# Three edits around the RWKV rounds of a hybrid encoder: a table of retention steps per round, a joint output norm of both token halves, and other tiles for the first output weights

## The chip, the cores and the metric

The kernel runs on one core of a Trainium2 chip. The metric is the device time of one execution in microseconds (us). Engines are named as in the profile: PE is TensorE (PEld its weight loads), ACT ScalarE, DVE VectorE, POOL GpSimd, SP SyncE, which here only issues DMAs.

## What is computed

Two layers. Each projects the normalised tokens, runs three groups of heads side by side (retention, RWKV-7, differential attention), multiplies the concatenated result by an output matrix and adds a SwiGLU. The change touches the end of the first two groups and the start of the output projection:

```python
for l in range(DEPTH):                                   # DEPTH = 2, 1024 tokens, 1024 features
    proj = rms_norm(x, mix_norm_g[l]) @ w_in[l]
    y_ret  = retention_mixer(...)    # head_group_norm(y_fwd + y_bwd) * silu(g), 6 heads of 64
    y_rwkv = rwkv7_mixer(...)        # a scan in each direction, then:
        # y = head_group_norm(ys[0] + flip(ys[1]), ln_w, ln_b)
        # return (y + bonus) * gate,   gate = sigmoid(xg @ g1) @ g2
    y_diff = diff_attention(...)
    x = x + concatenate([y_ret, y_rwkv, y_diff], -1) @ w_out[l]
    x = x + (silu(rms_norm(x) @ w_gate[l]) * (rms_norm(x) @ w_up[l])) @ w_down[l]

def head_group_norm(y, w, b, eps):   # over the 64 features of a head
    yn = (y - mean(y)) * rsqrt(mean((y - mean(y))**2) + eps)
    return yn * w + b
```

## The kernel before

Tokens lie along the free dimension in two halves of 512, features on 128 partitions, so a pair of heads fills a tile. Dense products are made of three matmuls each, with every operand split into a high part (ACT copies it, L185) and a low part (the rest, by DVE or POOL, L188).

**The rounds.** `rwkv` (L858) runs the RWKV scan of a layer in rounds w = -2 to 11. There are three pairs of heads, each with four blocks (two halves by two directions), so twelve blocks; round w runs the second half of block w and the first half of block w+1. A round has 16 slots, and eight recurrence steps start in it, one in every second slot (four in rounds -1 and 11). One step (`rwkv_rec`) hops between engines: PE makes `x`, ACT copies it to `U`, PE makes `ns`, ACT scales it to the new state `S`, PE adds to the output `y`. In the same slots the round advances generators "beside" the recurrence: products and inverses of later blocks (`rwkv_prep`, `rwkv_inv`, `rwkv_key`, `rwkv_ready`), the output norm `rwkv_fin` of a finished half, and the retention group `ret_all`. Each generator has a rate, in steps (`yield`s) per round; those but the retention are run out at the end of the round in one go. The retention keeps `RSTEP = 10` steps per round and takes 42 steps for each of its three pairs. At the end the program order of PE, ACT, DVE and POOL inside the rounds is fixed by dependencies, so each of these engines works its list in the written order; an instruction that waits holds all behind it.

**The norms.** `head_norm` (L808) squares `y` on ACT, sums over heads on PE (`vps`), and on ACT takes `Ln` and `Exp` with scale -0.5 for the reciprocal root; then DVE multiplies and ACT applies weight and bias (Identity). `Ln` and the other functions of the rounds use different tables of ACT, so a table load stands before and after each `Ln`. `head_norm` has two callers: the retention, once for each pair, with both halves (tiles `ryT`, `rt`), and `rwkv_fin` (L832), once for each pair and half (tiles `y`, `fq`). `rwkv_fin` also loads the bonus `bo` and the gate input `gl`, makes the gate on PE (`gps`), and writes the half to DRAM (`mixed`). Half 1 of pair p is normed in round 4p+3, half 0 in round 4p+4; the last half 0 comes after the rounds. The tiles `y`, `bo`, `gl` and the four of the bonus share a ring of four buffers.

**The output projection.** `out_blocks` (L1363) loads the eight rows of `mixed` for half 1, splits them (`mixl` to `hh` and `hl`), and works eight output blocks `cb` by both halves into PSUM tiles `aps`. The weights of blocks 0 and 1 are loaded by POOL's DMA queue into the tiles `wr` of pool W, split there by ACT (`whh`) and POOL (`wll`). W's memory is that of tiles the rounds use; `wr`'s load waits until those are read for the last time. Pool F (18 buffers of 128 x 512) holds the residual rows `x`.

Of the kernel before, what the change touches and what calls it, by code (L numbers as in the profile page):

```python
# [27 lines left out]
RSTEP = 10  # L28
# [149 lines left out]
class Net:  # L178
# [630 lines left out]
    def head_norm(self, y, eps, w, b, q):  # L809
# [14 lines left out]
        self.act(q, q, AF.Exp, scale=-0.5)  # L824
        yield
        for i in range(n):
            self.tt(q[:, sl[i]], y[i], q[:, sl[i]], ALU.mult)
            self.act(q[:, sl[i]], q[:, sl[i]], AF.Identity, scale=w, bias=b)

    def rwkv_fin(self, l, st, half):  # L830

        nc = self.nc  # L832
        p = st["p"]
        pp = self.par[l][:, P_PAIR + p * PP:P_PAIR + (p + 1) * PP]
        sl = slice(half * 512, half * 512 + 512)
        yield
        lg = self.Y.tile([128, 128], F32, tag="lg", name="lg")
        nc.sync.dma_start(out=lg, in_=self.ia["lora"][l, :, 1920 + p * 128:2048 + p * 128])
        bo = self.ring("bo")
        nc.sync.dma_start(out=bo, in_=self.bod[p][:, sl])  # L840
        gl = self.ring("gl")
        nc.sync.dma_start(out=gl, in_=self.lod[2][:, sl])
        q = self.Y.tile([128, 512], F32, tag="fq", name="fq", bufs=2)
        yield
        yield from self.head_norm([st["y"][half]], self.eps64, pp[:, Q_LNW:Q_LNW + 1], pp[:, Q_LNB:Q_LNB + 1], q)
        yield 1
        ps = self.bank([128, 512], "gps")
        self.mm(ps, lg, gl)
        self.tt(q, q, bo, ALU.add)
        yield  # L850
        self.tt(q, q, ps, ALU.mult)
        self.free(ps)
        nc.sync.dma_start(out=self.mixed[3 + p][:, sl], in_=q)

    def rwkv(self, l):
# [32 lines left out]
        ret = [self.ret_all(l), RSTEP, 0, 0]  # L888
        first = len(self.nc.cur_bb.bb.instructions)
        active, outs = [], []  # L890
        for w in range(-2, 12):
# [18 lines left out]
            if w >= 0 and j == 3:  # L910
                beside.append([self.rwkv_fin(l, sts[p], 1), 10, 0, 0])
            if w > 0 and j == 0:
                beside.append([self.rwkv_fin(l, sts[p - 1], 0), 10, 0, 0])
            if w > -2:
                beside.append(ret)
            else:
                next(ret[0])
# [34 lines left out]
        run(ret[0], self.rwkv_fin(l, sts[2], 0))  # L952
# [412 lines left out]
    def out_blocks(self, l):  # L1365
# [283 lines left out]
```

## Time and profile before

| what | us |
|---|---|
| median of three runs (3480.74 to 3483.1) | 3482.06 |
| the profiled execution, as timed | 3490.52 |
| its span, first to last instruction | 3488.7 |
| rounds of layer 0, round -1 to the last recurrence step | 572 to 950 |
| rounds of layer 1 | 2296 to 2671 |

The numbers of the views below are those of the profiled execution. A round is cut where ACT copies the first `U` of its recurrence steps. In a timeline row, the square bracket is the time in which the engine stood idle just before, and what ended it. PEclk is the clock that TensorE was granted, as a share of 2.4 GHz. A windows row gives start:end and length of the stretch, then the busy time of PE, PEld, DVE, ACT and POOL, each with its count of instructions, then PEclk, the busy share of the DMA engines and GB/s. The two layers run the same program; the rows below are of layer 1.

### The profile page before, as it was taken

The numbers are of one execution on the slowest core, as the hardware profiler recorded it, in microseconds if no ns is written. First come the engines' busy times: TensorE is split into PE (matmuls) and PEld (weight loads), VectorE is DVE, ScalarE is ACT, GpSimd is POOL, SyncE is SP. The second block draws the span as 40 slices with busy tenths as digits, with TensorE's granted clock in tenths as the row PEclk, the third lists the DMA queues.
The fourth block names the chain that finished last, engine by engine and source line by source line (L and its number), as shares of the span: only waits on it lengthen the run. The fifth ranks groups of instructions, "written<-read, shape, count | busy, mean of one in ns | idle before, by whom it ended". The sixth has DMA issues, their size and how long they took to land.

```text
span 3488.7 us, 71259 instructions
## 1 busy us (share of the span) xinstructions
PE 3209.4 (92%) x29148; PEld 2596.5 (74%) x29148; DVE 1994.8 (57%) x3805; ACT 1568.5 (45%) x2993; POOL 824.5 (24%) x724
## 2 busy tenths in 40 slices
PE   6999799988798999999989997998987999999997
PEld 4778587876676888878867776877766778887886
DVE  4699525676348555542338884176754585555433
ACT  4576444656534333332236664356555333333322
POOL 2222130000022545422122221200001144544220
PEclk9999799998899999999999998999988999999999
DMA  5454324433242222283044433344324322224721
GB/s 176 147 149 123 111 103 157 138 112 114 95 174 73 76 90 77 85 286 118 27 161 130 149 109 123 107 142 157 116 95 162 114 73 79 79 82 140 238 73 49
DMA packets 214928, 419.43 MB, mean 120 GB/s; under 512 B 23972, under 2 KB 59812, under 8 KB 214564
## 3 DMA queue, kind: packets, MB, share of 16 engines
q1 hardware_dynamic: 191288, 376.83, 32.8%
q0 software_dynamic: 10640, 14.95, 1.9%
q10 hardware_dynamic: 12672, 23.07, 1.7%
q8 instruction: 230, 3.77, 0.4%
q14 instruction: 98, 0.80, 0.1%
HBM read 314.06 MB, written 100.70 MB: 119 GB/s over the span
## 4 chain that ended last, share of the span: by engine, by line
PE 75%; DVE 11%; ACT 7%; DMA 3%; issue 2%; POOL 1%; SPq 0%; DVEq 0%; ACTq 0%; POOLq 0%
PE sp L194 22%; PE dps L194 14%; PE dn L194 13%; PE aps L194 5%; PE ns L194 2%; ACT L185 2%; PE y L194 2%; DMA wr<-in_w_in_dram 1%; PE pv L194 1%; PE tps L1247 1%; DVE pt L1217 1%; PE s L194 1%; PE btp L194 1%; PE pps L194 1%; PE yps L194 1%
## 5 line engine op out<-in xcount | busy, mean ns | idle before, releaser
L188 POOL TENSOR_TENSOR wll<-wr,whh 128x512 fp32r<-128x512 f32 x400 | 541.4, 1356 | 1452.7 <-ACT whh L185 1262.0
L185 ACT ACTIVATE whh<-wr 128x512 fp32r<-128x512 f32 x416 | 260.8, 630 | 643.2 <-PE dn L194 169.3
L194 PE MATMUL dps<-hh,whh 128*128 128x512 f32 x960 | 388.0, 405 | 0.5 <-ACT whh L185 0.3
L194 PE MATMUL dps<-hl,whh 128*128 128x512 f32 x960 | 384.4, 400 | 2.8 <-DVE hl L188 2.7
L194 PE MATMUL dps<-hh,wll 128*128 128x512 f32 x960 | 384.0, 400 | 0.7 <-POOL wll L188 0.6
L194 PE MATMUL sp<-hl,whh 128*128 128x512 f32 x704 | 278.6, 396 | 2.0 <-DVE hl L188 2.0
L194 PE MATMUL dn<-hh,whh 128*128 128x512 f32 x704 | 275.9, 392 | 4.6 <-ACT hh L185 4.6
L194 PE MATMUL dn<-hl,whh 128*128 128x512 f32 x704 | 277.0, 393 | 2.5 <-DVE hl L188 2.5
L194 PE MATMUL sp<-hh,whh 128*128 128x512 f32 x704 | 276.8, 393 | 1.8 <-ACT hh L185 1.4
L194 PE MATMUL dn<-hh,wll 128*128 128x512 f32 x704 | 275.6, 392 | 0.0
L194 PE MATMUL sp<-hh,wll 128*128 128x512 f32 x704 | 275.0, 391 | 0.0
L188 DVE TENSOR_TENSOR hl<-hidr,hh 128x512 fp32r<-128x512 f32 x144 | 137.5, 970 | 180.7 <-ACT hh L185 178.7
L194 PEld LDWEIGHTS dps<-hl,whh 128*128 128x128 f32 x960 | 183.8, 191 | 48.8 <-DVE hl L188 8.1
L194 PEld LDWEIGHTS dps<-hh,whh 128*128 128x128 f32 x960 | 184.1, 192 | 45.1 <-issue 4.4
L188 POOL TENSOR_TENSOR wll<-ws,whh 128x512 fp32r<-128x512 f32 x120 | 175.6, 1463 | 175.2 <-ACT whh L185 169.1
L194 PE MATMUL sp<-sh,whh 128*128 128x512 f32 x528 | 210.4, 398 | 6.8 <-ACT as L185 6.8
L194 PE MATMUL sp<-sl,whh 128*128 128x512 f32 x528 | 212.1, 402 | 3.0 <-DVE sl L188 2.8
L194 PEld LDWEIGHTS dps<-hh,wll 128*128 128x128 f32 x960 | 183.5, 191 | 39.7 <-issue 2.4
L194 PE MATMUL sp<-sh,wll 128*128 128x512 f32 x528 | 211.7, 401 | 0.0
L185 ACT ACTIVATE whh<-ws 128x512 fp32r<-128x512 f32 x132 | 83.4, 632 | 240.2 <-PE sp L194 138.0
L185 ACT ACTIVATE pt<-pt,mx 128x1024 f32<-128x1024 f32 x128 | 146.9, 1149 | 62.3 <-DVE mx L1221 59.9
L194 PEld LDWEIGHTS dn<-hh,whh 128*128 128x128 f32 x704 | 133.2, 189 | 33.3 <-ACT hh L185 5.4
(277 smaller groups left out, 7193.2 us busy)
## 6 DMA issues: line engine op xcount, KB each, us to landing
hidr<-hid SPq DMA_DIRECT2D x144, 256.0 KB, 5.3
bias<-t SPq DMA_DIRECT2D x64, 512.0 KB, 3.7
wr<-in_w_in_dram SPq DMA_DIRECT2D x120, 256.0 KB, 3.0
wr<-in_w_gate_dram SPq DMA_DIRECT2D x44, 512.0 KB, 3.7
wr<-in_w_up_dram SPq DMA_DIRECT2D x44, 512.0 KB, 3.2
wr<-in_w_down_dram SPq DMA_DIRECT2D x44, 512.0 KB, 4.1
pr<-st SPq DMA_DIRECT2D x56, 256.0 KB, 2.3
lo<-lod SPq DMA_DIRECT2D x48, 256.0 KB, 3.2
```

What stands on the lines that cost most here:

```text
L185: self.nc.scalar.activation(out=out, in_=in_, func=func, **kw)
L188: (eng or self.nc.vector).tensor_tensor(out=out, in0=a, in1=b, op=op)
L194: self.nc.tensor.matmul(out, lhsT, rhs, start=start, stop=stop, **kw)
L1217: nc.vector.tensor_tensor_reduce(out=pt[:, sl], in0=ps, in1=bias[:, sl], scale=1.0, scalar=mx[:, 0:1] if kh else -3.0e38, op0=ALU.add, op1 ...
L1247: nc.tensor.transpose(ps[:, n * 128:(n + 1) * 128], P[0][:, c * 128:(c + 1) * 128], self.ident)
```

## The change

Three edits:

1. The retention's rate becomes a table, `RSTEPS`, one entry for each round from -2 to 11: 10, 10, 9, 9, 8, 10, 12, 12, 12, 7, 20, 24, 8 from round -1 on. `head_norm` is cut into more steps (the `Exp` and the final products of each half have steps of their own), so a retention pair takes 45 steps.
2. `rwkv_fin` takes a tuple of halves. For pairs 0 and 1 both halves are normed together in round 4p+4; round 4p+3 has no norm. Pair 2 keeps its half 1 in round 11 and half 0 after the rounds. `fq` becomes one tile of 1024 columns; the gate matrix `lg` is loaded once for a pair; `bo` and `gl` of the second half are loaded after the first half is done.
3. In `out_blocks` the weights of output blocks 0 and 1 go to four tiles of pool F (`wf`, split to `fh` and `fl`), loaded by POOL's queue and split at a high priority.

```diff
-RSTEP = 10
+RSTEPS = (0, 10, 10, 9, 9, 8, 10, 12, 12, 12, 7, 20, 24, 8)
...
     def head_norm(self, y, eps, w, b, q):
...
             self.act(q[:, sl[i]], ps[i], AF.Ln, scale=1.0 / 64, bias=eps[:, 0:1])
             self.free(ps[i])
-        self.act(q, q, AF.Exp, scale=-0.5)
-        yield
         for i in range(n):
+            yield
+            self.act(q[:, sl[i]], q[:, sl[i]], AF.Exp, scale=-0.5)
+        for i in range(n):
+            yield
             self.tt(q[:, sl[i]], y[i], q[:, sl[i]], ALU.mult)
             self.act(q[:, sl[i]], q[:, sl[i]], AF.Identity, scale=w, bias=b)
 
-    def rwkv_fin(self, l, st, half):
+    def rwkv_fin(self, l, st, halves):
...
+        if halves[0]:
+            lg = st["lg"] = self.Y.tile([128, 128], F32, tag="lg", name="lg")
+            nc.sync.dma_start(out=lg, in_=self.ia["lora"][l, :, 1920 + p * 128:2048 + p * 128])
+            st["q"] = self.Y.tile([128, T], F32, tag="fq", name="fq")
...
+        ld = load(halves[0])
...
+        yield from self.head_norm([st["y"][half] for half in halves], self.eps64, pp[:, Q_LNW:Q_LNW + 1],
+                                  pp[:, Q_LNB:Q_LNB + 1], q)
+        for i, half in enumerate(halves):
+            bo, gl = ld if i == 0 else load(half)
+            t = q[:, i * 512:i * 512 + 512]
+            yield 1
+            ps = self.bank([128, 512], "gps")
+            self.mm(ps, lg, gl)
+            self.tt(t, t, bo, ALU.add)
+            yield
+            self.tt(t, t, ps, ALU.mult)
...
-            if w >= 0 and j == 3:
-                beside.append([self.rwkv_fin(l, sts[p], 1), 10, 0, 0])
+            if w == 11:
+                beside.append([self.rwkv_fin(l, sts[p], (1,)), 10, 0, 0])
             if w > 0 and j == 0:
-                beside.append([self.rwkv_fin(l, sts[p - 1], 0), 10, 0, 0])
+                beside.append([self.rwkv_fin(l, sts[p - 1], (1, 0)), 10, 0, 0])
             if w > -2:
+                ret[1] = RSTEPS[w + 2]
                 beside.append(ret)
...
+        raw = [self.F.tile([128, 4, 128], F32, tag="f", name="wf") for _ in range(4)]
+        for i, r in enumerate(raw):
+            nc.gpsimd.dma_start(out=r, in_=self.ia["w_out"][l, i // 2, :, i % 2 * 4:i % 2 * 4 + 4])
+        with self.tc.high_priority(offset=200000):
+            for i, r in enumerate(raw):
+                hi, lo = self.split(self.F, r, ("f", "f"), eng=nc.gpsimd)
+                w[i // 2] = w.get(i // 2, []) + [(hi[:, k], lo[:, k]) for k in range(4)]
         load(0)
-        for cb in range(2):
-            w[cb] = self.weights(self.ia["w_out"][l, cb], nc.gpsimd)
         load(1)
```

What this does to the order of the engines is shown at three places. The first is ACT in the middle of round 3, of layer 0: `e`, `cs`, `kd` and `WC` belong to the preparation of a later block, `S` and `U` to the recurrence. Before:

```order
L185 ACTIVATE cs<-cs 128x512
L185 ACTIVATE kd<-ta,der_127 128x512
L185 ACT_TABLE_LOAD
L185 ACTIVATE fq<-vps,eps_122 128x512
L185 ACT_TABLE_LOAD
L185 ACTIVATE fq<-fq 128x512
L185 ACTIVATE WC<-e_3467 128x8
L185 ACTIVATE S<-ns,WC 128x64
```

And now:

```order
L185 ACTIVATE cs<-cs 128x512
L185 ACTIVATE kd<-ta,der_127 128x512
L185 ACTIVATE rt<-rt 128x512
L185 ACTIVATE WC<-e_3467 128x8
L185 ACTIVATE S<-ns,WC 128x64
```

The norm of half 1 of pair 0 has left round 3; in its place stands one half's `Exp` of the retention's norm of pair 0, whose `Ln` now stands between the two `lw` at the start of this round and stood at the end of round 2.

The second is DVE from the last product of a round's preparation (`BP`) to the first part of the output sum `y` of round 4, layer 0: `rq`, `rsw` and `rQ` are the rotary products of the retention's pair 1, `N`, `NB`, `TB` and `YB` the inverse of a later block. Before:

```order
L188 TENSOR_TENSOR BP<-srp,c 128x8x64
L188 TENSOR_TENSOR rq<-rq,rsw 128x1024
L188 TENSOR_TENSOR rQ<-rq,rc 64x1024
L639 STREAM_TRANSPOSE N<-NB 128x8x32
L613 STREAM_TRANSPOSE NB<-N 128x1024
L188 TENSOR_TENSOR TB<-NB,YB 128x30
L188 TENSOR_TENSOR YB<-YB,TB 128x2x15
L188 TENSOR_TENSOR rQ<-rq,rc 64x1024
L188 TENSOR_TENSOR y<-y,yT 128x256
```

And now:

```order
L188 TENSOR_TENSOR BP<-srp,c 128x8x64
L639 STREAM_TRANSPOSE N<-NB 128x8x32
L613 STREAM_TRANSPOSE NB<-N 128x1024
L188 TENSOR_TENSOR TB<-NB,YB 128x30
L188 TENSOR_TENSOR YB<-YB,TB 128x2x15
L188 TENSOR_TENSOR rsw<-rsw,rope 128x1024
L188 TENSOR_TENSOR rq<-rq,rope 128x1024
L188 TENSOR_TENSOR y<-y,yT 128x256
```

Two wide products of the retention stand ahead of `y` where three stood.

The third is ACT from the last norm (half 0 of pair 2, behind the rounds) to the first split rows of the output projection, layer 0. Before:

```order
L185 ACTIVATE fq<-y 128x512
L185 ACT_TABLE_LOAD
L185 ACTIVATE fq<-vps,eps_122 128x512
L185 ACT_TABLE_LOAD
L185 ACTIVATE fq<-fq 128x512
L185 ACTIVATE fq<-fq,par_74 128x512
L185 ACTIVATE hh<-mixl 128x512 x6
L185 ACTIVATE whh<-wr 128x512
L185 ACTIVATE hh<-mixl 128x512
L185 ACTIVATE whh<-wr 128x512
```

And now:

```order
L185 ACTIVATE fq<-y 128x512
L185 ACT_TABLE_LOAD
L185 ACTIVATE fq<-vps,eps_122 128x512
L185 ACTIVATE fh<-wf 128x512
L185 ACT_TABLE_LOAD
L185 ACTIVATE fq<-fq 128x512
L185 ACTIVATE fh<-wf 128x512 x2
L185 ACTIVATE fq<-fq,par_74 128x512
L185 ACTIVATE fh<-wf 128x512
L185 ACTIVATE hh<-mixl 128x512 x13
```

The copies of the first weights stand inside the last norm, ahead of all `hh`.

## Rows read from the trace of the kernel before

**Rows 1.** The page: busy time by engine, and the chain that ended last.

```profile
PE 3209.4 (92%) x29148; PEld 2596.5 (74%) x29148; DVE 1994.8 (57%) x3805; ACT 1568.5 (45%) x2993; POOL 824.5 (24%) x724
PE 75%; DVE 11%; ACT 7%; DMA 3%; issue 2%; POOL 1%; SPq 0%; DVEq 0%; ACTq 0%; POOLq 0%
```

**Rows 2.** Windows, rounds 2 to 11 of layer 1: busy PE, PEld, DVE, ACT, POOL; clock.

```profile
2378.20:2410.70 32.50, 29.11 (x850) 24.71 (x846) 18.27 (x54) 22.66 (x53) 0.37 (x4) 1.00 0.48 157
2410.70:2443.00 32.30, 26.51 (x680) 21.63 (x684) 23.18 (x58) 22.27 (x53) 0.00 (x0) 0.89 0.57 175
2443.00:2481.00 38.00, 31.49 (x736) 26.42 (x728) 26.48 (x62) 21.70 (x54) 0.00 (x0) 0.87 0.30 93
2481.00:2509.80 28.80, 28.77 (x769) 24.43 (x765) 25.59 (x60) 16.28 (x47) 0.00 (x0) 1.00 0.35 114
2509.80:2542.40 32.60, 28.94 (x814) 25.46 (x814) 16.82 (x51) 18.30 (x50) 0.37 (x4) 0.97 0.51 171
2542.40:2580.20 37.80, 30.36 (x746) 23.59 (x740) 22.40 (x59) 26.99 (x57) 0.00 (x0) 0.89 0.31 95
2580.20:2609.20 29.00, 24.56 (x652) 21.56 (x646) 22.01 (x52) 16.05 (x41) 0.00 (x0) 0.88 0.18 60
2609.20:2637.70 28.50, 26.97 (x698) 24.19 (x696) 12.47 (x16) 9.66 (x32) 0.00 (x0) 0.94 0.17 59
2637.70:2653.20 15.50, 15.46 (x342) 13.99 (x338) 2.32 (x5) 5.00 (x19) 0.00 (x0) 1.00 0.22 70
2653.20:2671.20 18.00, 10.89 (x114) 6.29 (x108) 5.03 (x9) 13.82 (x22) 0.00 (x0) 0.72 0.20 64
```

**Rows 3.** Timeline of ACT, the norm in round 3.

```profile
2423.64 1.28 ACT L185 ACT_TABLE_LOAD   x1
2424.94 0.69 ACT L185 ACTIVATE fq<-vps,eps 128x512 f32<-128x512 f32 x1
2425.64 1.28 ACT L185 ACT_TABLE_LOAD   x1
...
2427.58 0.29 ACT L185 ACTIVATE S<-ns,WC 128x64 f32<-128x64 f32 x1
```

**Rows 4.** Timeline of PE, the first matmul after four of its waits.

```profile
2410.89 0.48 PE L194 MATMUL ns<-Vd,kT 64*64 64x64 f32 x4 [3.04 <-ACT S L185]
...
2427.92 0.48 PE L194 MATMUL ns<-Vd,kT 64*64 64x64 f32 x4 [3.25 <-ACT S L185]
...
2450.05 0.33 PE L194 MATMUL y3ps<-NB,N 32*32 32x32 f32 x8 [2.68 <-ACT NB L185]
...
2665.84 0.48 PE L194 MATMUL x<-S,AR 64*64 64x64 f32 x4 [4.22 <-ACT S L185]
```

**Rows 5.** Timeline of DVE at the start of round 4.

```profile
2442.01 0.69 DVE L188 TENSOR_TENSOR BP<-srp,c 128x512 f32<-128x512 f32 x1 [2.20 <-PE srp L194]
2442.62 1.22 DVE L188 TENSOR_TENSOR rq<-rq,rsw 128x1024 f32<-128x1024 f32 x1
...
2448.88 0.42 DVE L188 TENSOR_TENSOR y<-y,yT 128x256 f32<-128x256 f32 x1
```

**Rows 6.** Timeline of ACT, the retention's norm in round 7.

```profile
2551.74 1.06 ACT L185 ACTIVATE rt<-rt 128x1024 f32<-128x1024 f32 x1
2554.41 1.50 ACT L185 ACTIVATE rt<-rt,der 128x512 f32<-128x512 f32 x2
```

**Rows 7.** Timeline of PE, eight transposes of the retention.

```profile
2458.76 1.05 PE L194 MATMUL tps<-c,rv 128*128 128x128 f32 x8
```

**Rows 8.** Timelines of PE, ACT and DVE at the start of the output projection.

```profile
2684.70 0.80 PE L194 MATMUL aps<-hh,whh 128*128 128x512 f32 x1 [10.42 <-ACT whh L185]
2686.74 0.80 PE L194 MATMUL aps<-hh,wll 128*128 128x512 f32 x1 [0.82 <-POOL wll L188]
2678.59 0.69 DVE L188 TENSOR_TENSOR fq<-fq,gps 128x512 f32<-128x512 f32 x1
2684.16 8.26 DVE L188 TENSOR_TENSOR hl<-mixl,hh 128x512 fp32r<-128x512 f32 x7 [0.35 <-ACT hh L185]
```

More of the change, by code (lines that the diff above doesn't have):

```diff
@@ L834, in rwkv_fin, with load @@
         pp = self.par[l][:, P_PAIR + p * PP:P_PAIR + (p + 1) * PP]
-        sl = slice(half * 512, half * 512 + 512)
         yield
[L837 to L843, printed above, removed]
-        yield
[L845 to L853, printed above, removed]
+        if halves[0]:
+            lg = st["lg"] = self.Y.tile([128, 128], F32, tag="lg", name="lg")
+            nc.sync.dma_start(out=lg, in_=self.ia["lora"][l, :, 1920 + p * 128:2048 + p * 128])
+            st["q"] = self.Y.tile([128, T], F32, tag="fq", name="fq")
+        lg = st["lg"]
+        def load(half):
+            r = []
+            for name, src in (("bo", self.bod[p]), ("gl", self.lod[2])):
+                t = self.ring(name)
+                nc.sync.dma_start(out=t, in_=src[:, half * 512:half * 512 + 512])
+                r.append(t)
+            return r
+        ld = load(halves[0])
+        q = st["q"]
+        if len(halves) == 1:
+            q = q[:, halves[0] * 512:halves[0] * 512 + 512]
+        yield
+        yield from self.head_norm([st["y"][half] for half in halves], self.eps64, pp[:, Q_LNW:Q_LNW + 1],
[9 more added lines that the diff above has]
+            self.tt(t, t, ps, ALU.mult)
+            self.free(ps)
+            nc.sync.dma_start(out=self.mixed[3 + p][:, half * 512:half * 512 + 512], in_=t)
     def rwkv(self, l):
@@ L887, in rwkv @@
         self.rwkv_open2()
-        ret = [self.ret_all(l), RSTEP, 0, 0]
+        ret = [self.ret_all(l), 0, 0, 0]
         first = len(self.nc.cur_bb.bb.instructions)
@@ L951, in rwkv @@
                 left = [b for b in left if b[2] != -1]
-        run(ret[0], self.rwkv_fin(l, sts[2], 0))
+        run(ret[0], self.rwkv_fin(l, sts[2], (0,)))
         last = {}
```

## The prediction, made before the changed kernel ran

> **What bounds the kernel now.** I read the page first. PE is busy in 92% of the span and 75% of the chain that ended last is PE work [rows 1], so no edit can win more than the time in which PE stands idle, or runs at half clock because it stood idle. None of the three edits removes PE work: they move it, and they move what PE waits for. So the question is where, around the RWKV rounds, PE waits. For this I cut both layers into rounds and asked for busy times in each [rows 2]. The reader should see in each row the length less the PE time. Rounds 5 and 10 have none left (28.80 against 28.77, 15.50 against 15.46, clock 1.00): they are PE's. Rounds 2, 3, 4, 6, 7, 8, 9 and 11 have 3.39, 5.79, 6.51, 3.66, 7.44, 4.44, 1.53 and 7.11 us of idle time, together 39.9 of 293 us, and in most of them the clock is below 1.00 as well. At half clock a matmul takes twice as long, so a wait costs more than its own length: busy time is longer behind it too.
>
> Then I read what ends these waits, on PE's timeline. In rounds 2, 3 and 11 it is the state `S` of ACT: 3.04, 3.25 and 4.22 us [rows 4]. ACT is not full there (22.66 of 32.50, [rows 2]), but in a burst: in round 3 the first table load of the `fq` norm begins at 2423.64 and the next `S` at 2427.58 [rows 3], so for 3.94 us ACT does nothing for the recurrence. PE has about 0.7 us of other work in its list there and waits the remaining 3.25. In round 4 the wait of 2.68 has another cause [rows 4]: ACT makes `NB` late since ACT's list holds a transpose `yT` for DVE's `y`, and DVE reached `y` only at 2448.88, 6.87 us after `BP`, for it had three wide products of 1.22 us of the retention ahead of it [rows 5]. In round 7 the retention's norm of pair 1 is the burst: `Exp` 1.06 and two `Identity` of together 1.50, with table loads and two `Ln` ahead [rows 6].
>
> **The change, part by part, for one layer.** All terms are against the profiled execution (3490.52, span 3488.7), which lies 8.5 us above the median of 3482.06; I take the difference as given and subtract the sum from both.
>
> *Joint norms.* Of six `fq` norms four remain, so four table loads per layer go: 4 x 1.28 = 5.1 us of ACT [rows 3], none of it on PE's path by itself. What counts is the burst. It leaves rounds 3 and 7. In rounds 4 and 8 the burst gets longer by one `Ln` and one `Exp` of about 0.7 each, so some 1.4 us, the second `Exp` now being a step of its own and open to an `S` in between. In rounds 4 and 8 too, `bo` and `gl` of the second half are loaded only when the first half is finished, so the second gate product can stand in PE's list ahead of its data. No row shows this wait. Bounds: 0 where the list holds work ahead of it, and some 3 us, like the longest waits in mid-round [rows 4]; I take 1 in each of the two rounds, nearer to 0, since the first gate product and its DVE sum stand between.
>
> *Retention steps.* The table moves the end of the retention from round 11 into round 10: rounds 9 and 10 take 20 and 15 steps where they had 10 each. Of PE's work, twelve transposes leave round 4 and sixteen leave round 8, which come back in rounds 5 and 9: at 1.05 us for eight [rows 7] these are 1.6 and 2.1 us.
>
> Round by round, with the idle time of [rows 2] as the most that can come back, plus up to 1 us for the clock:
>
> - Round 2: `Ln`, `Exp` and `Identity` of the retention's norm no longer stand in one piece before the `S` that cost 3.04 [rows 4]. -2.5 (0 to -3.1).
> - Round 3: the 3.25 goes, but `Exp` and `Identity` of the retention come in, in single steps, and its `Ln` with two table loads may come just behind the round's start. -1.5 (+1 to -3.5).
> - Round 4: two wide products ahead of `y` where three stood: 1.2 of the 2.68 goes, and with it the late `NB`; the transposes that left make place for the second norm's sums and gate product. The fq burst stays. -2.5 (+1 to -6).
> - Round 5 is full on PE; what comes there costs its price. +1 (0 to +2).
> - Round 6: fewer `yT` waits, -0.5 (+0.5 to -1.5).
> - Round 7: both bursts gone (the `fq` norm to round 8, the retention's norm spread over slots): 7.44 idle. -4.5 (-1 to -7).
> - Round 8: the wait for `NB` stays as it is, the gate load is new. +1 (-1 to +3).
> - Round 9: 2.1 us of transposes, and the score and output products that go with them; only 1.53 is idle there. +3 (+1 to +5).
> - Rounds 10 and 11: PE is full in round 10, but 5 or so of the retention's steps and its last norm leave round 11, where two norms with four table loads made the wait of 4.22 and the clock of 0.72 [rows 2, 4]. -3 (+2 to -7).
>
> The rounds: -2.5 - 1.5 - 2.5 + 1 - 0.5 - 4.5 + 1 + 3 - 3 = -9.5.
>
> *First output weights.* PE's first `aps` starts at 2684.70 after 10.42 us without work, released by ACT's `whh`, and its third, 2.04 later, is held by POOL's `wll` [rows 8]. Layer 0 does the same. DVE's last product of the norm is at 2678.59 to 2679.28 [rows 8]; then the rows for half 1 only need their copies. The new tiles are free after round 9, so the weights land during round 10 and their copies stand inside the norm, in a gap of ACT while it waits for DVE. What is late next is the first PSUM bank, which is the gate product's and so is free after 2679.28, and the first `hh` and `hl`: 1 to 1.5 us more. Start at about 2680.8 instead of 2684.70, that is -3.9; I take -3.5, since POOL's `fl` run beside DVE's last products, and `hl`, which took 8.26 / 7 = 1.18 each beside POOL's `wll` where a DVE product without it took 0.69 [rows 8]. (-1.5 to -5.)
>
> The Trainium skill has a rule for this, "SBUF — State Buffer", section "Who interferes with whom": a DVE instruction with two inputs in SBUF contends with a GpSimd instruction that reads SBUF. The rows agree (1.18 against 0.69), and the rule speaks against the third edit: with `fl` now earlier, about three DVE products of the norm would be 0.5 longer each, which would make this term -2.0 instead of -3.5.
>
> Sum: -9.5 - 3.5 = **-13 per layer, -26 for two**: 3490.52 - 26 = 3464.5 for a profiled execution like this one, and 3482.06 - 26 = **3456** for the median.
>
> What a table load costs decides whether the four fewer are worth much. In the trace it takes 1.28 and the next ACTIVATE begins 0.02 behind its end [rows 3]. The Trainium skill ("ScalarE: Activation LUTs", section "What ACT_TABLE_LOAD costs") puts a drain of about 1380 ns beside each load, 2.66 us in all; by that eight fewer loads would free ACT for 21 us, not for 10.3. The rows do not show that drain, and I use 1.28.
>
> **The rivals.**
>
> *Give-back.* The waits in rounds 2, 3 and 7 go, but the work is only moved: the retention's norm meets another `S` in round 3, round 4 keeps its DVE backlog, and the fuller rounds 5 and 9 cost what the others win. For it: rounds 5 and 10 have no idle time, and 1.53 is little for round 9 [rows 2]. Against it: 7.44 of idle in round 7 has nothing left in the new order to cause it. Then the rounds bring -2 per layer and the output -3: -10 in all, 3472.
>
> *The retention becomes the bound in rounds 9 and 10 (slower).* A block of retention goes from PE (score) to DVE or ACT (mask, copies) and back to PE within a few steps. With 20 steps in the 16 slots of round 9 and 15 in the short round 10, the next PE product of the retention stands about one slot behind, and DVE's product in between takes 0.69 [rows 5, 8]. If PE waits a whole product in a step, and nothing else covers it, it costs 0.69: 35 steps are 24 us per layer. It eats the gain of 13 from 19 such steps on, and is over 0.2% slower from 24 on; with 27, 27 x 0.69 - 13 = +5.6 per layer, +11 in all: 3493. Against it: DVE is busy 12.47 of 28.50 us in round 9 and 2.32 of 15.50 in round 10, and ACT 9.66 and 5.00 [rows 2], so both answer at once, and the recurrence of PE lies between.
>
> *The output does not start earlier.* The copies of the weights wait for DMAs that land only in round 11 or later, or hold up ACT's norm. Then the output's term is 0: -19, 3463. For it: it is POOL's queue, behind whatever POOL does; against: POOL is idle in rounds 8 to 11 [rows 2].
>
> **How the numbers follow.** About 0.2% (7 us) is what a measurement of this kernel can tell from no change. Forecast, 3440 to 3466: 0.58. More than that, each term near its far end (sum below -42): 0.05. Output not earlier, 3463: 0.10. Give-back, 3466 to 3480: 0.20, of it 0.12 on the faster side of 3475 and 0.08 within 0.2%. Retention bound, 3489 and above: 0.07. Faster: 0.58 + 0.05 + 0.10 + 0.12 = 0.85; same 0.08; slower 0.07. The range leaves out the largest gains, the slower case and the weaker half of give-back: 3440 to 3475, with some 0.2 outside.
>
> **What would show it.** Rounds 2, 3, 4 and 7 of both layers shorter by 1.5 to 4.5 us; no `Ln` of `fq` in rounds 3 and 7; eight table loads fewer; PE waits for `S` of 3 us gone from rounds 2, 3 and 11. Round 9 longer by about 3 and still nearly full, with idle time there or in round 10 on `rM` or `rV` if the retention is the bound. PE waiting on a DMA of `gl` ahead of the second `gps` in rounds 4 and 8, some 1 us. The first `aps` 6.5 us or so behind its last work instead of 10.42, and no wait for POOL at the third. I would be wrong if the waits come back in other rounds at the same length (then ACT's bursts were not the cause but the recurrence's own chain), or if the second-half loads cost 3 us each time.

## The result, and the profile after

The changed kernel takes 3446.91 us (median of four runs, 3444.24 to 3448.31) where the kernel before takes 3482.58 (3480.74 to 3484.12): a ratio of 0.9898, 95% interval 0.9882 to 0.9913, or 36 us less. The forecast was 3456, 26 us less, with a range of 3440 to 3475. Three single executions in the experiments were slow ones and are left out of all ratios: one of the kernel before (7948.51), one of e2_joint (3679.34, its profiled one) and one of e9_pad (5246.62).

The profiled execution of the changed kernel was timed at 3444.24 with a span of 3442.5; that of before had a span of 3488.7. The two differ by 46.2 us, about 10 more than the medians, because the one of before lay 8.5 above its median and this one 2.7 below. The page of the changed kernel, to be set beside [rows 1]: busy time by engine, and the chain that ended last by engine.

```profile
PE 3190.4 (93%) x29148; PEld 2579.3 (75%) x29148; DVE 1988.0 (58%) x3805; ACT 1558.0 (45%) x2991; POOL 826.6 (24%) x728
PE 74%; DVE 12%; ACT 6%; DMA 4%; issue 2%; POOL 1%; SPq 1%; DVEq 0%; ACTq 0%; POOLq 0%
```

PE has as many instructions as before (29148). Of the 46.2 us, 27.2 are PE's idle time (3488.7 - 3209.4 = 279.3 against 3442.5 - 3190.4 = 252.1), and 19.0 are busy time: as many matmuls took less time, at a mean granted clock of 0.971 in place of 0.961. Windows of rounds 2 to 11 of layer 1 of the changed kernel (start:end, length, busy time of PE, PEld, DVE, ACT, POOL with counts, PEclk, DMA share, GB/s), beside [rows 2]:

```profile
2352.90:2383.20 30.30, 27.49 (x831) 24.12 (x828) 16.21 (x49) 18.45 (x49) 0.37 (x4) 1.00 0.54 178
2383.20:2412.30 29.10, 25.13 (x677) 21.30 (x676) 16.73 (x53) 22.30 (x53) 0.00 (x0) 0.94 0.28 89
2412.30:2445.00 32.70, 27.08 (x702) 20.80 (x701) 29.21 (x63) 22.81 (x55) 0.00 (x0) 0.95 0.44 137
2445.00:2476.10 31.10, 30.43 (x776) 26.25 (x774) 26.42 (x64) 17.50 (x49) 0.00 (x0) 1.00 0.47 147
2476.10:2505.80 29.70, 29.61 (x816) 26.17 (x810) 20.34 (x55) 17.08 (x47) 0.00 (x0) 1.00 0.42 139
2505.80:2536.20 30.40, 25.74 (x746) 22.11 (x742) 16.79 (x52) 23.47 (x55) 0.37 (x4) 0.94 0.32 106
2536.20:2564.70 28.50, 23.07 (x644) 19.58 (x638) 22.95 (x52) 17.16 (x44) 0.00 (x0) 0.88 0.26 87
2564.70:2599.20 34.50, 31.56 (x754) 27.43 (x752) 17.28 (x22) 11.54 (x35) 2.26 (x4) 1.00 0.35 111
2599.20:2618.90 19.70, 16.86 (x314) 14.27 (x310) 4.92 (x9) 11.62 (x29) 0.00 (x0) 0.91 0.24 87
2618.90:2629.00 10.10, 6.51 (x109) 4.05 (x104) 2.51 (x5) 6.69 (x13) 0.00 (x0) 1.00 0.16 52
```

Rounds 2, 3, 4 and 7 are shorter by 2.2, 3.2, 5.3 and 7.4 us, and round 9 is longer by 6.0, of which 4.6 are PE's own work (31.56 busy against 26.97). From the first recurrence step of the rounds to the last, the layers take 357.9 and 354.1 us against 376.7 and 373.7.

Most of the gain lies where the prediction looked. From the first `U` of round 2 to the last `U`, both kernels run the same 6296 matmuls in each layer. PE's idle time there fell by 10.6 us in layer 0 (40.5 to 29.9) and by 7.5 in layer 1 (39.6 to 32.1), and its busy time by 6.4 (255.0 to 248.6) and 9.6 (252.5 to 242.9), while the mean clock rose from 0.91 to 0.93 and from 0.92 to 0.96.

The start of the output projection of layer 1, on PE, POOL and DVE, beside [rows 8]. Since the last `U`, 10.2 us have passed at the first `aps` where 14.4 had; in layer 0 it is 9.8 for 13.4. The third `aps` waits no more.

```profile
2638.09 0.76 PE L194 MATMUL aps<-hh,fh 128*128 128x512 f32 x1 [4.74 <-ACT hh L185]
2639.49 0.63 PE L194 MATMUL aps<-hh,fl 128*128 128x512 f32 x1
2635.28 4.70 POOL L188 TENSOR_TENSOR fl<-wf,fh 128x512 fp32r<-128x512 f32 x3 [1.15 <-ACT fh L185]
2636.46 0.69 DVE L188 TENSOR_TENSOR fq<-fq,bo 128x512 f32<-128x512 f32 x1 [1.05 <-DMA mixl<-mix]
2637.26 0.69 DVE L188 TENSOR_TENSOR fq<-fq,gps 128x512 f32<-128x512 f32 x1
2637.86 8.69 DVE L188 TENSOR_TENSOR hl<-mixl,hh 128x512 fp32r<-128x512 f32 x12
```

Of these twelve `hl`, the first two, beside the last `fl`, took 0.98 and 1.77 us, and the other ten 0.68 each. The seven of before in [rows 8] are of two kinds as well: the four beside POOL's `wll` took 1.40 to 1.77, the other three 0.68, and 1.18 is the mean of both.

### The profile page after: what moved, and what is told of

Its sections match the earlier page's. It is cut to its first block, busy times and chain, and to the rows that moved or that the text cites. A ratio compares the mean times of both kernels' runs of the same rounds, so it can differ in the third digit from the quotient of the medians.

```text
span 3442.5 us, 71253 instructions
## 1 busy us (share of the span) xinstructions
PE 3190.4 (93%) x29148; PEld 2579.3 (75%) x29148; DVE 1988.0 (58%) x3805; ACT 1558.0 (45%) x2991; POOL 826.6 (24%) x728
## 4 chain that ended last, share of the span: by engine, by line
PE 74%; DVE 12%; ACT 6%; DMA 4%; issue 2%; POOL 1%; SPq 1%; DVEq 0%; ACTq 0%; POOLq 0%
PE sp L194 23%; PE dps L194 14%; PE dn L194 14%; PE aps L194 4%; PE ns L194 2%; PE y L194 2%; DMA wr<-in_w_in_dram 2%; PE pv L194 1%; PE tps L1265 1%; DVE pt L1235 1%; PE s L194 1%; ACT L185 1%; DVE hl L188 1%; PE yps L194 1%; PE btp L194 1%
## 5 line engine op out<-in xcount | busy, mean ns | idle before, releaser
L188 POOL TENSOR_TENSOR wll<-wr,whh 128x512 fp32r<-128x512 f32 x392 | 529.6, 1353 | 1440.8 <-ACT whh L185 1242.5
L194 PEld LDWEIGHTS dps<-hh,wll 128*128 128x128 f32 x960 | 182.8, 190 | 40.5 <-POOL wll L188 3.1
L194 PEld LDWEIGHTS sp<-hl,whh 128*128 128x128 f32 x704 | 132.6, 188 | 34.2 <-DVE hl L188 5.5
```

The source lines that it names most:

```text
L188: (eng or self.nc.vector).tensor_tensor(out=out, in0=a, in1=b, op=op)
L194: self.nc.tensor.matmul(out, lhsT, rhs, start=start, stop=stop, **kw)
```

## The experiments

What is asked is which of the edits makes the 36 us, and by what. Theory A, that of the prediction: the table and the joint norms take bursts of ACT out of the rounds that wait, each edit on its own account. Theory B: the edits only pay together. Each kernel is compared with the kernel before on the same chip; a gain below is one less the ratio of the table, times 3482 us.

| kernel | median us | ratio to before, 95% interval | gain us |
|---|---|---|---|
| changed kernel | 3446.91 | 0.9898 (0.9882 to 0.9913) | 36 |
| e1_ret: edit 1 alone | 3457.43 | 0.9933 (0.9920 to 0.9946) | 23 |
| e2_joint: edit 2 alone | 3472.18 | 0.9969 (0.9957 to 0.9980) | 11 |
| e3_out: edit 3 alone | 3474.99 | 0.9984 (0.9974 to 0.9995) | 6 |
| e4_flat: all, table flat at 10 | 3443.89 | 0.9892 (0.9875 to 0.9909) | 38 |
| e5_fine: the norm's finer steps alone | 3451.05 | 0.9917 (0.9905 to 0.9929) | 29 |
| e6_table: the table alone | 3479.64 | 1.0005 (0.9996 to 1.0013) | -2 |
| e9_pad: three empty steps | 3475.93 | 0.9985 (0.9976 to 0.9994) | 5 |
| e8_mix: all, other table, earlier loads | 3446.55 | 0.9898 (0.9884 to 0.9911) | 36 |
| e10_fine_out: finer steps and edit 3 | 3442.19 | 0.9887 (0.9874 to 0.9900) | 39 |
| e11_fine_ret: finer steps, retention only | 3468.88 | 0.9961 (0.9947 to 0.9975) | 14 |
| e12_fine_fin: finer steps, RWKV norms only | 3463.51 | 0.9944 (0.9931 to 0.9957) | 19 |
| e13_best: e10 with 12 steps in rounds 10, 11 | 3449.77 | 0.9907 (0.9894 to 0.9919) | 32 |

The length of the rounds of layer 1 in the profiles (each cut where ACT copies the first `U` of the round, the last where it copies the last one), and in the last column the time from there to the first `aps`. Each row is one profiled execution; layer 0 mostly differs by less than 2 us in a round, but round 5 of e5_fine is 34.8 there and round 7 of e9_pad 40.7:

| round | 2 | 3 | 4 | 5 | 6 | 7 | 8 | 9 | 10 | 11 | to `aps` |
|---|---|---|---|---|---|---|---|---|---|---|---|
| before | 32.5 | 32.3 | 38.0 | 28.8 | 32.6 | 37.8 | 29.0 | 28.5 | 15.5 | 17.1 | 14.4 |
| changed | 30.3 | 29.0 | 32.8 | 31.1 | 29.7 | 30.4 | 28.5 | 34.5 | 19.7 | 9.0 | 10.2 |
| e5_fine | 30.4 | 27.7 | 37.6 | 28.8 | 29.6 | 34.6 | 26.2 | 25.9 | 16.0 | 11.4 | 20.4 |
| e11_fine_ret | 30.7 | 32.8 | 37.0 | 28.7 | 29.7 | 42.8 | 24.4 | 25.8 | 16.0 | 11.3 | 20.0 |
| e12_fine_fin | 32.8 | 27.3 | 36.5 | 28.8 | 32.0 | 32.6 | 28.5 | 28.3 | 15.5 | 16.5 | 14.7 |
| e9_pad | 32.6 | 32.2 | 35.9 | 29.0 | 30.1 | 44.2 | 27.6 | 25.9 | 16.0 | 11.3 | 19.9 |
| e6_table | 29.9 | 37.3 | 34.5 | 33.7 | 34.4 | 36.2 | 27.5 | 32.5 | 18.5 | 11.2 | 14.3 |
| e4_flat | 30.6 | 23.0 | 37.0 | 32.3 | 29.7 | 30.5 | 30.2 | 27.4 | 16.0 | 11.4 | 17.6 |
| e10_fine_out | 30.4 | 27.7 | 38.3 | 29.0 | 29.4 | 35.8 | 23.9 | 26.5 | 16.0 | 11.4 | 17.6 |

**One edit at a time.**

e1_ret is the kernel before with the table and the finer steps of `head_norm`:

```diff
-RSTEP = 10
+RSTEPS = (0, 10, 10, 9, 9, 8, 10, 12, 12, 12, 7, 20, 24, 8)
...
+            self.act(q[:, sl[i]], q[:, sl[i]], AF.Exp, scale=-0.5)
```

> Edit 1 alone: the table of retention steps and the finer steps of the shared norm; the RWKV norms stay one half at a time, and the output weights stay where they were. Theory A (the edits remove separate waits and their gains add up): round 7 loses its 3.5 us burst of the retention's norm, rounds 2 and 4 lose part of theirs, round 11 loses the retention's norm, round 9 grows by 3 to 6; about -14 us in all, 3468. Theory B (the edits need each other: the low rates 8 and 7 in rounds 4 and 8 are only worth something where a joint norm fills the room): within 0.2% of before, 3476 to 3489, with the fq bursts of rounds 3 and 7 still followed by waits of 3 us for S.

It gave 23 us, more than either theory said. Theory B falls with it.

e2_joint is the kernel before with the new `rwkv_fin` and its calls:

```diff
-                beside.append([self.rwkv_fin(l, sts[p - 1], 0), 10, 0, 0])
+                beside.append([self.rwkv_fin(l, sts[p - 1], (1, 0)), 10, 0, 0])
```

> Edit 2 alone: both halves of pairs 0 and 1 normed together in rounds 4 and 8, retention at 10 steps in every round as before, output weights as before. Theory A: the wait of 3.25 us in round 3 goes in both layers, round 7 loses its fq burst, rounds 4 and 8 get longer by 1 to 3 us: about -8 us in all, 3474. Theory B: rounds 4 and 8 now hold two halves' norm beside 10 retention steps, they grow by as much as rounds 3 and 7 lose: same as before, 3480 to 3488.

11 us, near theory A's 8. Only its times are used here.

e3_out is the kernel before with the weights in pool F:

```diff
+        raw = [self.F.tile([128, 4, 128], F32, tag="f", name="wf") for _ in range(4)]
...
-            w[cb] = self.weights(self.ia["w_out"][l, cb], nc.gpsimd)
```

> Edit 3 alone: the first output weights in four tiles of pool F. Both theories: it touches nothing in the rounds; the stretch from the last recurrence step to the first aps falls from 13.4 and 14.4 us to about 10 in each layer, and the wait for wll of about 1 us goes: -8 us in all, 3474. If the copies delay the last norm instead, 0.

6 us (2 to 9). The profile shows the mechanism as forecast: 9.7 and 10.8 us from the last `U` to `aps` for 13.4 and 14.4. The parts sum to 23 + 11 + 6 = 40 for a whole of 36, so they nearly add up, as theory A has it. But theory A's reason for the largest part had still to be tried.

e4_flat is the changed kernel with a flat table:

```diff
-RSTEPS = (0, 10, 10, 9, 9, 8, 10, 12, 12, 12, 7, 20, 24, 8)
+RSTEPS = (0,) + (10,) * 13
```

> All three edits but a flat table, 10 retention steps in every round (the finer steps of the norm are kept). Against the changed kernel (3446.9), Theory A: rounds 9 and 10 get their old lengths back (about 6 and 4 us shorter per layer), but round 11 gets the retention's tail and a last norm with table loads (8 longer), and rounds 4 and 8 hold the joint norm beside more retention: about 5 us per layer slower, 3457. Theory B (the table is what makes the joint norm pay): most of the gain is lost, 3470 or more.

Neither: 3443.89, not slower at all. The table brings nothing here. With it fell the reason that the prediction gave for its terms of rounds 4, 9, 10 and 11: that the retention's steps move away from the rounds that wait.

**What in edit 1 does it.** What was left of edit 1 was the cut of `head_norm` into more steps, which both its callers use.

e5_fine is the kernel before with `head_norm` alone changed:

```diff
-        self.act(q, q, AF.Exp, scale=-0.5)
-        yield
         for i in range(n):
+            yield
+            self.act(q[:, sl[i]], q[:, sl[i]], AF.Exp, scale=-0.5)
+        for i in range(n):
+            yield
             self.tt(q[:, sl[i]], y[i], q[:, sl[i]], ALU.mult)
```

> The kernel before with only the finer steps of head_norm (a retention pair takes 45 steps instead of 42, at 10 steps a round as before; one half's RWKV norm takes two steps more). Edit 1 alone gave -24 us, all three edits with a flat table -37, and edits 2 and 3 alone -9 and -6. Theory C (the finer steps do the work of edit 1, the table nothing): -22 us, 3459. Theory D (table and finer steps each bring about half): -12 us, 3469.

e6_table is the kernel before with the table alone, `head_norm` as it was:

```diff
-RSTEP = 10
+RSTEPS = (0, 10, 10, 9, 9, 8, 10, 12, 12, 12, 7, 20, 24, 8)
...
             if w > -2:
+                ret[1] = RSTEPS[w + 2]
                 beside.append(ret)
```

> The kernel before with only the table of rates; head_norm in its old, whole steps, 42 for a retention pair, so all retention ends earlier than in the changed kernel. Theory C: within 5 us of before, 3476 to 3486. Theory D: -12 us, 3469.

The finer steps alone give 29 us, the table alone -2 (-4.5 to 1.4). Theory C holds. The table on top of the finer steps (e1_ret) is some 6 us worse in the median than the finer steps alone, but the two intervals overlap, so that the difference is not shown.

In the RWKV norms the finer steps add one thing: a `yield` between `Ln` and `Exp`. It is one step more for a half, not two as the expectation said. Here is ACT in round 3 of e5_fine, to be set beside [rows 3]:

```profile
2401.12 1.28 ACT L185 ACT_TABLE_LOAD   x1
2402.42 0.69 ACT L185 ACTIVATE fq<-vps,eps 128x512 f32<-128x512 f32 x1
2403.00 0.20 ACT L185 ACTIVATE WC<-e 128x8 f32<-128x8 f32 x1
2403.11 0.30 ACT L185 ACTIVATE S<-ns,WC 128x64 f32<-128x64 f32 x1
2403.31 0.22 ACT L185 ACTIVATE U<-x 128x64 f32<-128x64 f32 x1
2403.55 1.28 ACT L185 ACT_TABLE_LOAD   x1
2404.84 0.63 ACT L185 ACTIVATE fq<-fq 128x512 f32<-128x512 f32 x1
```

The norm is still in round 3 with both its table loads. But `S` stands after 1.99 us, between the two, not after 3.94 behind both. Not every wait fell in e5_fine: round 4 is hardly shorter, since DVE waits 3.32 us there for the retention's load of `rsw`, and PE 7.03 us for `NB`.

**Whose finer steps.** Here `head_norm_fine` is the new `head_norm` and `head_norm` the old one. e11_fine_ret uses the new one in the retention alone:

```diff
-        yield from self.head_norm(yh, self.eps5, dd[:, 6:7], dd[:, 7:8], q)
+        yield from self.head_norm_fine(yh, self.eps5, dd[:, 6:7], dd[:, 7:8], q)
```

> The kernel before with the finer steps only in the retention's norm (two halves: five stretches on ACT instead of two); the RWKV norms keep Ln and Exp in one stretch. If each wait is worth what it showed in the trace of before: the wait of 3.04 in round 2 and that of 3.5 to 4.2 in round 7 go, with the time at half clock behind them, and the shift by three steps brings the 5 us that empty steps alone brought: -18 us, 3463. The waits of 3.25 in round 3 and 2.04 in round 4 stay.

And e12_fine_fin in the RWKV norms alone:

```diff
-        yield from self.head_norm([st["y"][half]], self.eps64, pp[:, Q_LNW:Q_LNW + 1], pp[:, Q_LNB:Q_LNB + 1], q)
+        yield from self.head_norm_fine([st["y"][half]], self.eps64, pp[:, Q_LNW:Q_LNW + 1], pp[:, Q_LNB:Q_LNB + 1], q)
```

> The kernel before with the finer steps only in the RWKV norms: one step more, between Ln and Exp, so that an S can stand between the two table switches; the retention's norm and its 42 steps stay. The waits of 3.25 in round 3, 2.04 in round 4 and of about the same in rounds 7 and 8 shrink to 1 to 1.5: -10 us, 3471. If a burst cut in two delays S as much as before (the second half meets the next S): 3478 to 3484.

e9_pad is the kernel before with the retention's 45 steps but the old bursts:

```diff
         yield from self.head_norm(yh, self.eps5, dd[:, 6:7], dd[:, 7:8], q)
         yield
+        yield
+        yield
+        yield
```

> The kernel before with three empty steps behind each retention norm: a pair takes 45 steps as in the changed kernel, so that what follows is started as late as there, but the norm itself is in whole steps as before. If what the finer steps bring is the shorter bursts on ACT (Exp and Identity of one half each): within 5 us of before, 3476 to 3486. If it is the shift of the later pairs against the rounds (other work meets the same recurrence): as the finer steps alone, about -20 us, 3460.

14, 19 and 5 us; 14 + 19 = 33 for the 29 of both. e12_fine_fin gained twice what was expected, and e9_pad stayed within some 5 us, as its first case has it. Below is PE's wait for `S` behind the RWKV norm in the middle of round 3, in e11_fine_ret, e12_fine_fin and e9_pad; the second row of e11_fine_ret and of e9_pad is the longest wait in round 7 (a [bracket] is the idle time before the matmul and what ended it):

```profile
2406.30 0.27 PE L194 MATMUL ns<-Vd,kT 64*64 64x64 f32 x2 [4.18 <-ACT S L185]
2540.59 0.48 PE L194 MATMUL ns<-Vd,kT 64*64 64x64 f32 x4 [3.85 <-ACT S L185]
```

```profile
2408.65 0.33 PE L194 MATMUL ns<-Vd,kT 64*64 64x64 f32 x4 [1.41 <-ACT S L185]
```

```profile
2415.62 0.37 PE L194 MATMUL ns<-Vd,kT 64*64 64x64 f32 x2 [3.33 <-ACT S L185]
2554.00 0.37 PE L194 MATMUL ns<-Vd,kT 64*64 64x64 f32 x2 [6.21 <-ACT S L185]
```

Where the RWKV norm is cut, the wait in round 3 is 1.41 and the round 27.3 us long; where it is not, 4.18 and 3.33, and 32.8 and 32.2. In round 7 of e12_fine_fin, too, an `S` stands between the two loads of the RWKV norm, and the round is 32.6 long. An RWKV norm with an empty step at another place was not run; that e12_fine_fin's 19 us come from the cut and not from a shift of what follows rests on this: of its 14.4 us in the rounds of layer 1, 10.2 lie in rounds 3 and 7.

e11_fine_ret did not do as expected in the rounds. Of the waits that were to go, that of 3.04 went, but the one in round 7 stayed (3.85 for 3.50) and the round grew to 42.8; and the two that were to stay grew, from 3.25 to 4.18 in round 3 and from 2.04 to 3.35 in round 4. How much of its 14 us is the shorter bursts and how much the shift by three steps is open, since the empty steps of e9_pad do not bring the shift alone. The wait of 6.21 is what the empty steps made: the retention's norm of pair 1 now stands directly behind the RWKV norm of round 7. ACT there, in e9_pad:

```profile
2544.77 1.28 ACT L185 ACT_TABLE_LOAD   x1
2546.06 0.69 ACT L185 ACTIVATE fq<-vps,eps 128x512 f32<-128x512 f32 x1
2546.77 1.28 ACT L185 ACT_TABLE_LOAD   x1
2548.06 0.63 ACT L185 ACTIVATE fq<-fq 128x512 f32<-128x512 f32 x1
2548.71 1.28 ACT L185 ACT_TABLE_LOAD   x1
2550.00 1.26 ACT L185 ACTIVATE rt<-vps,eps 128x512 f32<-128x512 f32 x2
2551.29 1.28 ACT L185 ACT_TABLE_LOAD   x1
2552.58 1.06 ACT L185 ACTIVATE rt<-rt 128x1024 f32<-128x1024 f32 x1
2553.54 0.20 ACT L185 ACTIVATE WC<-e 128x8 f32<-128x8 f32 x1
2553.65 0.29 ACT L185 ACTIVATE S<-ns,WC 128x64 f32<-128x64 f32 x1
```

From the first load to the next `S` it is 8.88 us, and round 7 is 44.2 long instead of 37.8 (in layer 0, 40.7 instead of 37.8). ACT does the same work as before in that round or the ones beside it; in one piece it costs 3 to 6 us more. The 5 us that the empty steps gain come from other rounds (round 6 from 32.6 to 30.1, and rounds 9 and 11, from which the retention's last steps moved out behind the rounds, where they cost 5.5 of it again).

**What the other two edits add to the finer steps.**

e10_fine_out is the kernel before with the edits of e5_fine and e3_out together:

```diff
-        self.act(q, q, AF.Exp, scale=-0.5)
-        yield
...
+            yield
+            self.act(q[:, sl[i]], q[:, sl[i]], AF.Exp, scale=-0.5)
...
+        raw = [self.F.tile([128, 4, 128], F32, tag="f", name="wf") for _ in range(4)]
```

> The finer steps of head_norm and the new output weights, at 10 retention steps a round, and every RWKV norm of one half by itself as before. The finer steps alone gave -30 us, the output weights alone -6, and with the joint norms added to both -37. If the joint norm is worth nothing once the norms are cut into steps (they cure the same waits): -36 us, 3445. If it is worth its 9 us there too, and something else was lost when the three came together: then this is -28, 3453.

39 us. It has neither joint norms nor a table and is as fast as the changed kernel (0.9887 against 0.9898, intervals that overlap widely) and as e4_flat, which is the same with the joint norms added (0.9892). So the joint norm's 11 us are there only as long as the norms stand in whole bursts; once they are cut, it adds nothing. In layer 1 it then moves time about: against e10_fine_out, rounds 3 and 7 of e4_flat are shorter by 4.7 and 5.3 us, and rounds 5 and 8, where its work comes back, longer by 3.3 and 6.3.

One part of this is seen in e4_flat: PE waits for the gate input of the second half, in round 8 of each layer.

```profile
2568.67 1.15 PE L194 MATMUL gps<-gl,lg 128*128 128x512 f32 x1 [3.37 <-DMA gl<-lod]
```

e8_mix tried to take this away, together with the retention's tail behind the rounds. It is the changed kernel with:

```diff
-RSTEPS = (0, 10, 10, 9, 9, 8, 10, 12, 12, 12, 7, 20, 24, 8)
+RSTEPS = (0, 10, 10, 10, 10, 10, 10, 10, 10, 10, 10, 14, 14, 8)
...
+        lds = [ld] + [load(half) for half in halves[1:]]
         for i, half in enumerate(halves):
-            bo, gl = ld if i == 0 else load(half)
+            bo, gl = lds[i]
```

> All three edits with the table flat at 10 up to round 8, then 14, 14 and 8, so that the retention ends inside round 11 and not behind it; and bo and gl of the second half are loaded as soon as the norm has read y, ahead of the first half's gate product. With the flat table the start of the output came 17.6 us after the last recurrence step (9.8 and 10.2 in the changed kernel), and PE waited 3.4 us on gl in round 8. If both waits go and nothing takes their place: 5 to 10 us per layer, of which 1 to 3 are given back in rounds 9 to 11: 3432. If round 9 and 10 pay for the moved steps in full: 3444, as with the flat table.

It paid in full: 3446.55. The load of `bo` went as soon as DVE had read `y`, but that of `gl` was issued only behind PE's first gate product, for which SyncE's queue waited 4.7 us, and PE's wait stayed (3.42). The way to the first `aps` fell from 17.6 to 9.5, and rounds 9, 10 and 11 grew from 54.8 to 63.4 in layer 1. The same was tried with e10's norms. e13_best is e10_fine_out with:

```diff
-RSTEP = 10
+RSTEPS = (0,) + (10,) * 11 + (12, 12)
```

> As the finer steps with the new output weights, but 12 retention steps in rounds 10 and 11, so that no retention stands behind the rounds. With 10 in each, the output came 20 us after the last recurrence step, 7 to 10 us later than with none behind it. If round 10 and 11 take the four steps into waits that they have anyway: -4 us against its sister with 10, 3441. If they pay in full, as the moved steps did before: the same, 3445.

3449.77, slower than e10 by some 7 us, with intervals that overlap by a little. From the last `U` to `aps` it is 11.0 in place of 17.6, but round 11 is 16.8 long in place of 11.4 and round 10 17.3 in place of 16.0. Four steps, the retention's last norm, cost as much among four recurrence steps that wait on ACT as behind them. No version beat the changed kernel by more than the intervals; e10_fine_out equals it with fewer edits.

## Why the prediction was right, and where it was not

The direction, the place and the range were right, and so was the cause in general: ACT's bursts of table loads ahead of an `S`. The sum was too small, since it had next to nothing for the clock, and the account of which edit does it was wrong.

- **Whom the gain was booked to.** The prediction saw what finer steps do for the retention's norm (round 2, "no longer stand in one piece"; round 7, "spread over slots"). For the RWKV norms it had only "the second `Exp` now being a step of its own", and gave the gain of rounds 3 and 7 to joint norms that leave them and that of rounds 4 and 11 to the table. The runs show the reverse: finer steps 29 us, and 19 with those of the RWKV norms alone; table -2; joint norms nothing on top of the finer steps. The step that failed is the reading of [rows 3]: 3.94 us were taken as one thing that has to be moved elsewhere, when a slot for one `S` in its middle does nearly as well (1.41 of wait left in e12_fine_fin, 2.24 in e5_fine).
- **The table loads.** Eight fewer came as forecast (65 for 73; eight take 10.2 us of ACT, not 10.3), but their number is not what pays: e12_fine_fin has 73 and gains 19 us, and e10_fine_out has 69 and is as fast as the changed kernel.
- **"Round 4: the `fq` burst stays."** It did not stay as a burst. ACT in round 4 of the changed kernel:

```profile
2429.39 1.28 ACT L185 ACT_TABLE_LOAD   x1
2430.68 1.26 ACT L185 ACTIVATE fq<-vps,eps 128x512 f32<-128x512 f32 x2
2431.84 0.21 ACT L185 ACTIVATE WC<-e 128x8 f32<-128x8 f32 x1
2431.95 0.31 ACT L185 ACTIVATE S<-ns,WC 128x64 f32<-128x64 f32 x1
2432.14 0.23 ACT L185 ACTIVATE U<-x 128x64 f32<-128x64 f32 x1
2432.39 1.28 ACT L185 ACT_TABLE_LOAD   x1
2433.68 0.63 ACT L185 ACTIVATE fq<-fq 128x512 f32<-128x512 f32 x1
```

  And PE's first matmul behind that `S`:

```profile
2432.31 0.33 PE L194 MATMUL ns<-Vd,kT 64*64 64x64 f32 x4 [1.11 <-ACT S L185]
```

  Although it norms two halves, the wait for that `S` is 1.11 (2.04 before). The round fell by 5.2, not 2.5, but only 0.9 of it is idle time (6.51 to 5.62). The rest is busy time (31.49 to 27.08): the clock was 0.95 for 0.87, and 24 transposes and 16 `sps` of the retention left the round, where the prediction counted twelve transposes. The transposes come back in round 5, as the 24 that left round 8 (it counted sixteen) do in round 9.
- **The clock.** This is the term of the sum that was mis-sized most: "up to 1 us" in a round, and next to nothing in the -9.5. In rounds 2 to 11 idle time fell by 10.6 and 7.5 us in the two layers, about what the sum said, and busy time by 6.4 and 9.6 more, on the same 6296 matmuls at a higher clock. Over the whole program 19 of 46 us were busy time. Round 3 of e12_fine_fin has nearly the same work in it as before (22 small matmuls, some 0.3 us, fall into the next round); it is 5.0 us shorter, 3.6 of it idle time (5.79 to 2.15) and 1.4 busy time (26.51 to 25.15; clock 0.89 to 0.94, [rows 2] and the row below). A wait also drags others behind it: the 1.84 us that the wait for `S` itself lost is half of the 3.6.

```profile
2393.40:2420.70 27.30, 25.15 (x658) 20.01 (x660) 22.59 (x58) 22.28 (x53) 0.00 (x0) 0.94 0.52 170
```

- **Round by round**, layer 1, forecast and measured: round 2 -2.5, -2.2; 3 -1.5, -3.3; 4 -2.5, -5.2; 5 +1, +2.3; 6 -0.5, -2.9; 7 -4.5, -7.4; 8 +1, -0.5; 9 +3, +6.0; 10 and 11 -3, -3.9. Round 1 and those before, which the sum left out, gave -2.5. Every term but that of round 8 had the right sign, and most were too small: -9.5 became -19.6 in the profiles (-18.8 in layer 0). Round 2 hit its number partly by luck: the wait of 3.04 is gone, but others stand in its place (1.27 for `U`), so that only 0.6 of the 2.2 is idle time, and four wide `vps` moved on to round 3. Against the medians, whose difference is 36 and not 46, it is less. Which rounds of the profiled execution of before hold its extra 8.5 us is open. Round 6 goes with the shift by three steps that the longer norm brings, not with the bursts: in layer 1 it is 29.4 to 30.1 long in every kernel with 45 steps for a retention pair, the empty ones of e9_pad too, and 32.0 to 34.4 in the others.
- **The waits for `NB`.** In round 4, one wide product fewer was to bring `y` forward and take 1.2 off the wait of 2.68. `y` stands 5.60 us behind `BP` in the changed kernel, where it stood 6.87 behind it [rows 5]. The wait itself is 2.99, but an idle 1.55 us that stood a little ahead of it is gone: from the start of the round to `y3ps`, PE's idle time fell from 4.24 to 2.99, by the 1.2 that was forecast. The wait in round 8 was to stay; it is 4.99, and was 4.12. On DVE, and then on PE (the first and the last row are these two waits):

```profile
2411.54 0.69 DVE L188 TENSOR_TENSOR BP<-srp,c 128x512 f32<-128x512 f32 x1 [1.70 <-PE srp L194]
2417.14 0.41 DVE L188 TENSOR_TENSOR y<-y,yT 128x256 f32<-128x256 f32 x1
```

```profile
2418.30 0.26 PE L194 MATMUL y3ps<-NB,N 32*32 32x32 f32 x8 [2.99 <-ACT NB L185]
2525.09 0.48 PE L194 MATMUL ns<-Vd,kT 64*64 64x64 f32 x4 [2.93 <-ACT S L185]
2543.02 0.33 PE L194 MATMUL y3ps<-NB,N 32*32 32x32 f32 x8 [4.99 <-ACT NB L185]
```

  The middle row is the retention's norm of pair 1 in round 7, of whose wait 2.93 of 3.50 is left: the second table load, `e`, `cs`, `kd` and one of the two `Exp` still stand between two `S` there. The round is shorter by 7.4 all the same: the RWKV norm has left it, the wait of 1.48 for `N` is gone, and PE is busy for 25.74 us in place of 30.36.
- **The second half's gate load**, priced at 1 us in rounds 4 and 8, cost PE no wait for a DMA in the changed kernel and 3.4 in round 8 of e4_flat: the bound of 3 was about right. The two kernels differ in the order of the retention's steps alone.
- **The output**: -3.5 forecast per layer, -4.2 and -3.6 in the profiles, 6 us for both layers when alone. The contention feared there did not cost DVE's norm anything: both products beside POOL's `fl` took 0.69, though the first (`fq` and `bo`) has two inputs in SBUF. The `fl` that started during it took 1.79, where the two ahead of it took 1.25 and 1.27. The two `hl` that overlapped an `fl` took 0.98 and 1.77, the other ten 0.68. The rule of the Trainium skill ("SBUF — State Buffer", section "Who interferes with whom"), that a DVE instruction with two inputs in SBUF contends with a GpSimd instruction that reads SBUF, agrees with these rows, and the first product shows that it need not be DVE that takes longer.
- **The rivals.** The give-back did not come for the whole, but it did for the joint norms on top of the finer steps, as said above. The retention as the bound of rounds 9 and 10 came in part: 10 us more there in layer 1 (54.2 against 44.0), of which 6.0 are PE's own work and 4.2 idle time (1.57 to 5.78, [rows 2] and the windows above), and round 11 (9.0 for 17.1) and the way to `aps` (10.2 for 14.4) gave it back. The idle time is not on `rM` or `rV`. The longest part is a new wait for `S` in round 10: with 24 retention steps in 16 slots, both table loads, the two `Ln` and both `Exp` of the last retention norm stand between two `S` again, for all their steps. On PE, and then ACT's first load and next `S`:

```profile
2613.40 0.48 PE L194 MATMUL ns<-Vd,kT 64*64 64x64 f32 x4 [2.67 <-ACT S L185]
2608.12 1.28 ACT L185 ACT_TABLE_LOAD   x1
...
2613.05 0.30 ACT L185 ACTIVATE S<-ns,WC 128x64 f32<-128x64 f32 x1
```

  e1_ret has the same wait of 2.67; e5_fine, whose last retention norm comes later, has none in round 10. So the high rate undoes there what the finer steps do elsewhere, which goes with the table being worth nothing: e4_flat has 27.4 and 16.0 us in rounds 9 and 10, 17.6 on the way to `aps`, and takes as long in all.

## What to carry to other kernels

Where a chain of small steps and bulky work share one in-order engine, look first for the longest stretch of that engine without a step of the chain, and cut it at its natural seams before moving it: one more place to switch, between the two table loads, was worth more (19 to 29 us) than moving the work, batching it or retuning the rates. Test the parts of an edit apart, its incidental ones too; here the detail made most of the gain, and the table and the joint norms added nothing that could be measured once it was there. And price a wait at PE with the stretch at the lower clock behind it: busy time was two fifths of the gain here.

## What the runs showed of the hardware

A switch of tables on ACT took 1.28 us and no more: in all of the stretches shown, the next instruction begins 0.01 or 0.02 us behind its end. That makes `Ln` and `Exp` of a norm of 512 columns 3.88 us on ACT, of which 2.56 are switches, and four instructions of ACT enough to hold PE for 3 us. PE paid again behind it: the first `ns` behind the 3.25 wait took 0.48 where it took 0.33 behind the wait of 1.41. In the kernel before, the granted clock fell to 0.5 (1.2 GHz) 0.16 us before the end of the long wait, and the stretch of 8 us after it ran at 0.80 of 2.4 GHz on average; a stretch of 8 us in e12_fine_fin, behind the wait of 1.41, ran at 1.00 and held 204 matmuls for 148. The two rows, before and e12_fine_fin:

```profile
2428.00:2436.00 8.00, 7.54 (x148) 6.58 (x150) 5.83 (x14) 3.13 (x9) 0.00 (x0) 0.80 0.43 136
2409.00:2417.00 8.00, 7.63 (x204) 7.17 (x200) 6.71 (x15) 6.70 (x15) 0.00 (x0) 1.00 0.48 151
```
